# Rotary scores on one core: which ring carries the loads of q and k

## The chip, the cores and the metric

The kernel runs on one core of a Trainium2 chip. The core has five engines that run on their own: TensorE (PE, matrix products and transposes), VectorE (DVE), ScalarE (ACT), GpSimd (POOL) and SyncE (SP, which here only issues transfers). Transfers between the chip's memory (HBM) and the on-chip tiles are carried by 16 DMA engines. An engine that issues a transfer puts it on a ring of its own: in the profile q1 is SyncE's, q10 ScalarE's and q0 GpSimd's. All three are served by the same 16 DMA engines.

The metric is the device time of one execution in microseconds (us); lower is better. Three runs of the kernel before gave 802.26, 803.96 and 805.82 us; the median is 803.96.

## What is computed

q and k have the shape (16, 512, 16, 64): batch, position, head, dimension, in 32-bit floats. Both are rotated by cosines and sines of the position, and for each batch and head all scores of q against k are returned:

```python
q_rot = np.concatenate([q1 * cos_q - q2 * sin_q,
                        q1 * sin_q + q2 * cos_q], axis=-1)
k_rot = np.concatenate([k1 * cos_q - k2 * sin_q,
                        k1 * sin_q + k2 * cos_q], axis=-1)
scores = np.einsum('bshd,bthd->bsht', q_rot, k_rot)
```

q1, q2, k1 and k2 are the two halves of the last dimension. The output has the shape (16, 512, 16, 512): 268.44 MB are written and 67.24 MB read.

## The kernel before

**Tiling.** The 512 positions of a batch are laid on 128 partitions, four to a partition (C = 4): position 4p + c stands on partition p in row c. The work is cut into NST = 64 steps, four to a batch; step i computes, for batch i // 4 and row i % 4, the scores of 128 positions of q with all 512 of k, for all 16 heads. These go into one stage tile (`st`, 128 partitions of 32 KB, 4 MB), of which there are three (NST_BUFS), used in turn. When the eight head pairs of a step are copied there, one 4 MB store writes the tile out.

**A step** (the loop at L488, from the fifth step on). For each head pair p, `scores` (L396) records two matrix products (L413) into a PSUM tile `ps`, one of three, and ScalarE's copy of it into the stage tile (L422). Between them stand, for rows that later steps need, the transposes on TensorE (L364) of rotated q (one step ahead) and k (four steps, one batch, ahead), with the copies out of PSUM (L382): q's by VectorE after p = 1 and 3, k's by ScalarE after p = 5 and 6. VectorE rotates in place in the input tiles, q two steps ahead and k five (`rope`, L316, instructions at L339). The first four steps handle batch 0 in small pieces, with stores of 1 MB.

**Input tiles.** q and k have two tiles each of 128 partitions by 16 KB (2 MB, a whole batch), used in turn: batch b goes into tile b % 2. A load may begin when the rows that it overwrites have been read by TensorE's transposes. For k of batch b + 2 that is by the end of step 4b - 1, the last one of batch b - 1; for q of batch b + 2 it is in step 4b + 2 for the last row.

**The loads before.** From the fifth step on SyncE issues a load of q or k as two of 1 MB, each holding two of the four rows, with a semaphore of its own: `load(which, b, half)` at L264. The calls stand at the ends of the steps, behind the step's store: the first half of k after step 4b - 1, its second after step 4b, the halves of q after steps 4b + 1 and 4b + 2 (L486 and L511 to L518). So each step puts a 4 MB store and a 1 MB load on SyncE's ring, where they are served in that order. The loads of k and q for batches 1 and 2 (L445, L446 and L479) are whole.

**The four GpSimd loads.** RELIEVED (L260) names four loads of q, of batches 5, 8, 11 and 14. GpSimd issues 120 partitions of these, in packets of 8 KB, and the rest of eight partitions goes on SyncE's ring (for two of them) or GpSimd's (for the other two). They are issued after steps 14, 26, 38 and 50, when TensorE has read the rows.

**What sets the order.** Every operation is recorded in a list by `Plan.add`; `Plan.resolve` (L38) works out which semaphores each must wait for, and `Plan.emit` (L96) writes each engine's program in recorded order. An operation of an engine therefore starts after the earlier ones of that engine, and a DMA issue holds up what follows it on the issuing engine. All transfers go through `dma` (L236), whose `dma_start` the profile shows as L237, whatever engine issues. The engine is the first argument; waits that the issuing engine knows to be over are left out.

Of the kernel before, what the change touches and what calls it, by code (L numbers as in the profile page):

```python
# [7 lines left out]
PE, ACT, DVE, POOL, SP = "PE", "ACT", "DVE", "POOL", "SP"  # L8
# [170 lines left out]
def kernel(  # L179
# [8 lines left out]
    nc = tc.nc  # L188
# [4 lines left out]
    B, S, H, D = q.shape  # L193
    HD = D // 2
    P = 128
    C = S // P
# [9 lines left out]
    dram = {  # L206
        "q": q.rearrange("b (p c) h d -> b p c h d", c=C),
        "k": k.rearrange("b (p c) h d -> b p c h d", c=C),
    }
# [19 lines left out]
    def one(f):  # L229
        def emit():  # L230
            a = f()
            return a, a

        return emit

    def dma(engine, e, dst, src, sem, reads=(), writes=(), also=()):  # L236
        plan.add(engine, one(lambda: e.dma_start(dst, src)), reads, writes, sem=sem, also=also)  # L237
# [22 lines left out]
    RELIEVED = {("q", 5): 0, ("q", 8): 1, ("q", 11): 2, ("q", 14): 3}  # L260
    tiny = [0]
    SLOW = 4

    def load(which, b, half=None):  # L264
        if b >= B:
            return
        t = inb[which][b % 2]
        sem = f"in_{which}{b % 2}"
        rows = [("in", which, b % 2, c) for c in range(C)]
        rest = [("in rest", which, b % 2, c) for c in range(C)]  # L270
        if (which, b) not in RELIEVED:
            lo, hi = (0, C) if half is None else (half * C // 2, (half + 1) * C // 2)
            dma(
                SP, nc.sync, t[:, lo:hi].rearrange("p c (h d) -> p c h d", h=H), dram[which][b][:, lo:hi],
                sem if half is None else f"{sem}_{half}", writes=rows[lo:hi] + rest[lo:hi],
            )
            return

        n, E, F = 120, C * H * D, C * H * D // 2
        x = RELIEVED[which, b]
        d = dram[which][b]

        def move_cursor(k):
            y = tiny[0]
            tiny[0] += 1
            src = bass.AP(q.tensor, 512 * y, [(512, k), (64, 2), (1, 2)])
            dst = scratch[:k, 4 * y : 4 * y + 4].rearrange("p (a b) -> p a b", a=2)  # L290
            dma(POOL, nc.gpsimd, dst, src, "cursor", writes=[("scratch", y)])

        def halves(lo, hi, keys, sem):
            src = bass.AP(d.tensor, d.offset + lo * E + F, [(E, hi - lo), (-F, 2), (1, F)])
            v = t[lo:hi]
            dst = bass.AP(v.tensor, v.offset + F, [(v.ap[0][0], hi - lo), (-F, 2), (1, F)])
            dma(POOL, nc.gpsimd, dst, src, sem, writes=keys)

        plan.add(POOL, None, (), rows)
        if x % 2:  # L300
            move_cursor(8)
            halves(n, P, rest, f"rest{x}")
        move_cursor(SLOW + 1)
        halves(0, n, rows, f"part{x}")
        if not x % 2:
            dma(SP, nc.sync, t[n:].rearrange("p c (h d) -> p c h d", h=H), d[n:], sem, writes=rest)
# [9 lines left out]
    def rope(which, n):  # L316
        if n < C:
            x = units[which, n]
            sv, k1, k2 = "p c (g j) -> p c g j", {"j": HD}, {"j": D}
            cs = cos_t.unsqueeze(2).to_broadcast((P, C, 2 * G, HD))  # L320
            ss = ss_v.unsqueeze(2).to_broadcast((P, C, G, D))
            pv = part.rearrange("p (c g j) -> p c g j", c=C, j=D)
            x5 = x.rearrange("p c (h x j) -> p c h x j", x=2, j=HD)
            p5 = part.rearrange("p (c h x j) -> p c h x j", c=C, x=2, j=HD)
            adds = [(x5[:, :, :, y], p5[:, :, :, 1 - y]) for y in range(2)]
        else:
            x = inb[which][n // C % 2][:, n % C]
            sv, k1, k2 = "p (g j) -> p g j", {"j": HD}, {"j": D}
            cs = cos_t[:, n % C].unsqueeze(1).to_broadcast((P, 2 * H, HD))
            ss = ss_v[:, n % C].unsqueeze(1).to_broadcast((P, H, D))  # L330
            pv = part.rearrange(sv, **k2)
            x4 = x.rearrange("p (h x j) -> p h x j", x=2, j=HD)
            swapped = bass.AP(part.tensor, part.offset + HD, [part.ap[0], (D, H), (-HD, 2), (1, HD)])
            adds = [(x4, swapped)]
        xs, xc = x.rearrange(sv, **k2), x.rearrange(sv, **k1)
        keys, more = src_keys(which, n), src_also(which, n)

        def tt(o, a, b, op, reads, writes):
            plan.add(DVE, one(lambda: nc.vector.tensor_tensor(o, a, b, op=op)), reads, writes, also=more)  # L339

        def products():
            tt(pv, xs, ss, mult, keys + ["ss"], ["part"])
            tt(xc, xc, cs, mult, keys + ["cos"], keys)

        def sums():
            for y, z in adds:
                tt(y, y, z, add, keys + ["part"], keys)

        return [products, sums]
# [34 lines left out]
    def stage_of(i):  # L384
        return i % 2 if i < C else (i - 2) % NST_BUFS
# [4 lines left out]
    def ps_of(i, p):  # L390
        m = HP * i + p if i < FIRST else HP * ((i - FIRST) % PERIOD) + p
        if i >= FIRST and m >= HP * PERIOD - 3:
            return (1, 2, 1)[m - (HP * PERIOD - 3)]
        return m % NPS

    def scores(i, p):  # L396
        y, s = ps_of(i, p), stage_of(i)
        ps, st = ps_s[y], stage[s]
        b = i // C
        if b == 0:  # L400
            c, hp = divmod(p, 2)
            lhs, rhs = qTb[i % 2][:, C * hp + c], kTb[0][:, 2 * i + hp]
            keys = [("qT", i % 2, C * hp + c)] + [("kT", 0, 2 * i + hp, x) for x in range(C)]
        else:
            lhs, rhs = qTb[i % 2][:, p], kTb[b % 2][:, p]
            keys = [("qT", i % 2, p)] + [("kT", b % 2, p, x) for x in range(C)]

        def emit():
            done = []
            for r in range(2):  # L410
                lo, hi = 64 * r, 64 * r + 64
                done.append(
                    nc.tensor.matmul(out=ps[:, r, :], lhsT=lhs[lo:hi, :], rhs=rhs[lo:hi, :], start=True, stop=True)  # L413
                )
            return done[0], done[-1]

        plan.add(PE, emit, keys, [("ps", y)])
        so, si = st[:, 2 * p : 2 * p + 2, :], ps
        if b > 0:
            so = so.rearrange("s r (t c) -> s r t c", c=C)  # L420
            si = si.rearrange("s r (c t) -> s r t c", c=C)
        plan.add(ACT, one(lambda: nc.scalar.copy(out=so, in_=si)), [("ps", y)], [("st", s, p)])  # L422
        if b == 0 and p % 2 == 1:
            c = p // 2
            dma(
                SP, nc.sync, o_v[0, c, :, G * i : G * (i + 1)], st[:, G * c : G * (c + 1)], f"out{s}_{c}",
                reads=[("st", s, p - 1), ("st", s, p)],
            )
        elif b > 0 and p == HP - 1:
            dma(SP, nc.sync, o_v[b, i % C], st, f"out{s}", reads=[("st", s, x) for x in range(HP)])  # L430
# [5 lines left out]
    def run(ops):  # L436
        for op in ops:
            op()
# [3 lines left out]
    for head, heads in ((0, G), (G, H - G)):  # L442
        load_units("k", head, heads)
        load_units("q", head, heads)
    load("k", 1)  # L445
    load("q", 1)  # L446
    plan.add(POOL, one(lambda: nc.gpsimd.memset(ident, 0.0)), (), ["ident"])
    plan.add(
# [15 lines left out]
    for i in range(C):  # L464
# [18 lines left out]
                dve = dve[m:]  # L483
                tr_act(*nxt.pop(0))
        run(dve)
    load("k", 3, 0)  # L486

    for i in range(C, NST):  # L488
        plan.step = i
        tr = {}  # L490
        if i + 1 < NST:
            tr[1], tr[3] = ("q", i + 1, 0), ("q", i + 1, 1)
        if i + C < NST:
            tr[5], tr[6] = ("k", i + C, 0), ("k", i + C, 1)
        dve = []
        if i + 2 < NST:
            dve += rope("q", i + 2)
        if i + 1 + C < NST:
            dve += rope("k", i + 1 + C)
        for p in range(HP):  # L500
            scores(i, p)
            if p not in tr:
                continue
            if tr[p][0] == "q":
                run(dve[:1])
                dve = dve[1:]
                transposed(*tr[p], DVE)
            else:
                transposed(*tr[p], ACT)
        run(dve)  # L510
        if i % C == 0:  # L511
            load("k", i // C + 2, 1)
        elif i % C == C - 1:
            load("k", i // C + 3, 0)
        elif ("q", i // C + 2) not in RELIEVED:
            load("q", i // C + 2, i % C - 1)
        elif i % C == C - 2:
            load("q", i // C + 2)  # L518

    plan.resolve()  # L520
# [34 lines left out]
```

## Time and profile before

| What | Value | Where from |
|---|---|---|
| Time, three runs | 802.26, 803.96, 805.82 us | times |
| The profiled execution: time, span | 802.26 us, 800.5 us | times, page |
| Mean granted TensorE clock | 0.945 of full speed | times |
| TensorE busy (matrix products) | 680.5 us, 85% | page, part 1 |
| ScalarE busy | 561.6 us, 70% | page, part 1 |
| VectorE busy | 545.2 us, 68% | page, part 1 |
| DMA, whole span | 335.88 MB, mean 420 GB/s | page, part 3 |
| SyncE waiting for ScalarE's copies | 714.4 us, 76 times | waits of SyncE's queue |
| SyncE waiting for the last store | 21.1 us | waits of SyncE's queue |

The page's second part cuts the span in 40 slices of 20 us. A digit there is the busy share of an engine in tenths; the row DMA is the mean of the 16 DMA engines, and the row GB/s what they moved. The chain of waits (part 4) follows the work that ended last back to its cause, step by step. In the list of groups (part 5) a line ends with the idle time just before its instructions and what ended it. Part 6 gives for each kind of transfer the number, the size and the median time from issue to landing.

The trace also holds every DMA packet with queue, size and duration. The large ones of the kernel before:

```
queue         packet, bytes  packets  median ns  what
SyncE (q1)    32768          7680     1213       stores of 4 MB
SyncE (q1)    16384          528      612        whole loads, and small rests
SyncE (q1)    8192           7680     309        half loads; stores of 1 MB
GpSimd (q0)   8192           992      309        the four loads of q
```

### The profile page before, as it was taken

To read this page: it belongs to the slowest core of one execution; us is meant where nothing else is said; L and a number is where in the kernel's file an instruction comes from. 1 tells how busy PE (TensorE), PEld (TensorE's weight loads), DVE (VectorE), ACT (ScalarE), POOL (GpSimd) and SP (SyncE) were. 2 spreads that over 40 slices of the span, in tenths; PEclk is the share of its full clock that TensorE was granted. 3 is DMA by queue.
4 is the path that set the end of the run, shared out by engine and by line. 5 is a ranking of instruction groups with operands and counts; after the bars stand their busy time and mean duration, and the time that the engine had idled before them with its cause. 6 is when DMAs were issued, how large, how long until landed. Compare 5 with 4: busy or idle time off the path is not lost.

```text
span 800.5 us, 8241 instructions
## 1 busy us (share of the span) xinstructions
PE 680.5 (85%) x3072; PEld 292.0 (36%) x3072; DVE 545.2 (68%) x516; ACT 561.6 (70%) x647; POOL 8.4 (1%) x18
## 2 busy tenths in 40 slices
PE   3989999889699898869998988798889879989960
PEld 2444443334243333324343333343333324334420
DVE  6999988657487686648866765587767648775300
ACT  2978887867488668658786684687766658768870
POOL 0000000000000000100000000000000100000000
PEclk9999999989899999989999998899999989999995
DMA  9999999999999999999999999999999999999997
GB/s 350 419 424 414 386 436 421 438 424 401 429 429 430 436 428 434 389 436 431 430 431 432 429 432 383 432 432 428 434 433 427 380 438 427 431 432 426 433 431 306
DMA packets 21682, 335.88 MB, mean 420 GB/s; under 512 B 2480, under 2 KB 3760, under 8 KB 4784
## 3 DMA queue, kind: packets, MB, share of 16 engines
q1 hardware_dynamic: 20000, 327.43, 96.5%
q0 software_dynamic: 1376, 8.13, 2.8%
q10 hardware_dynamic: 288, 0.13, 0.1%
q8 instruction: 6, 0.10, 0.0%
q14 instruction: 12, 0.10, 0.0%
HBM read 67.24 MB, written 268.44 MB: 419 GB/s over the span
## 4 chain that ended last, share of the span: by engine, by line
DMA 52%; PE 31%; DVE 8%; ACT 5%; issue 1%; ACTq 0%; DVEq 0%; SPq 0%
DMA out_dram<-st 51%; PE ps L413 24%; PE bank L364 8%; ACT st L422 5%; DVE st L339 3%; DVE part L339 2%; DVE k_sb L339 2%; DVE q_sb L339 1%; DMA sin_t<-in_sin_dram 1%; DVE kT L382 0%; DVE qT L382 0%; ACTq L237 0%; ACT ss_t L459 0%; ACT ss_t L458 0%; ACTq L110 0%
## 5 line engine op out<-in xcount | busy, mean ns | idle before, releaser
L422 ACT COPY st<-ps 128x1024 f32<-128x1024 f32 x512 | 494.6, 1020 | 200.0 <-DMA out_dram<-st 124.8
L413 PE MATMUL ps<-kT,qT 64*128 64x512 f32 x2048 | 540.0, 641 | 77.9 <-ACT st L422 77.8
L413 PEld LDWEIGHTS ps<-kT,qT 64*128 64x128 f32 x2048 | 179.3, 193 | 269.4 <-ACT st L422 139.1
L382 DVE COPY qT<-bank 128x512 f32<-128x512 f32 x118 | 81.6, 692 | 199.5 <-PE bank L364 199.5
L364 PEld LDWEIGHTS bank<-ident,q_sb 128*128 128x128 f32 x480 | 54.0, 148 | 99.3 <-issue 94.3
L364 PE MATMUL bank<-ident,q_sb 128*128 128x128 f32 x480 | 84.6, 302 | 1.0 <-DVE q_sb L339 1.0
L364 PEld LDWEIGHTS bank<-ident,k_sb 128*128 128x128 f32 x480 | 50.4, 141 | 94.1 <-DVE k_sb L339 45.9
L364 PE MATMUL bank<-ident,k_sb 128*128 128x128 f32 x480 | 78.7, 287 | 1.6 <-DVE qT L382 0.8
L382 ACT COPY kT<-bank 128x512 f32<-128x512 f32 x122 | 72.7, 599 | 6.7 <-PE bank L364 6.7
L339 DVE TENSOR_TENSOR part<-q_sb,ss_t 128x1024 f32<-128x1024 f32 x60 | 73.5, 1225 | 3.7
L339 DVE TENSOR_TENSOR q_sb<-q_sb,cos_t 128x1024 f32<-128x1024 f32 x60 | 73.5, 1225 | 2.1
L339 DVE TENSOR_TENSOR k_sb<-k_sb,part 128x1024 f32<-128x1024 f32 x60 | 73.5, 1225 | 2.1
L339 DVE TENSOR_TENSOR k_sb<-k_sb,cos_t 128x1024 f32<-128x1024 f32 x60 | 73.5, 1225 | 2.0
L339 DVE TENSOR_TENSOR part<-k_sb,ss_t 128x1024 f32<-128x1024 f32 x60 | 73.0, 1216 | 0.3
L339 DVE TENSOR_TENSOR q_sb<-q_sb,part 128x1024 f32<-128x1024 f32 x60 | 72.9, 1216 | 0.0
L364 PE MATMUL bank<-ident,st 128*128 128x128 f32 x64 | 10.8, 318 | 14.2 <-DVE st L339 14.2
L364 PEld LDWEIGHTS bank<-ident,st 128*128 128x128 f32 x64 | 8.2, 161 | 19.5 <-DVE st L339 17.7
L339 DVE TENSOR_TENSOR part<-st,ss_t 128x1024 f32<-128x1024 f32 x8 | 9.8, 1223 | 7.4 <-ACT ss_t L459 7.0
L339 DVE TENSOR_TENSOR st<-st,part 128x512 f32<-128x512 f32 x16 | 11.1, 691 | 0.5
L237 POOL DMA_DIRECT2D scratch<-in_q_dram x6 | 3.6, 601 | 617.0 <-PE bank L364 617.0
L339 DVE TENSOR_TENSOR st<-st,cos_t 128x1024 f32<-128x1024 f32 x8 | 9.8, 1225 | 0.3
L382 ACT COPY qT<-bank 128x512 f32<-128x512 f32 x10 | 5.7, 618 | 3.5 <-PE bank L364 3.5
(11 smaller groups left out, 11.0 us busy)
## 6 DMA issues: line engine op xcount, KB each, us to landing
out_dram<-st SPq DMA_DIRECT2D x60, 4096.0 KB, 25.7
k_sb<-in_k_dram SPq DMA_DIRECT2D x26, 1024.0 KB, 28.6
q_sb<-in_q_dram SPq DMA_DIRECT2D x18, 1024.0 KB, 27.2
out_dram<-st SPq DMA_DIRECT2D x16, 1024.0 KB, 12.0
q_sb<-in_q_dram POOLq DMA_DIRECT2D x4, 1920.0 KB, 30.9
k_sb<-in_k_dram SPq DMA_DIRECT2D x2, 2048.0 KB, 13.7
q_sb<-in_q_dram SPq DMA_DIRECT2D x2, 2048.0 KB, 15.4
st<-in_k_dram SPq DMA_DIRECT2D x1, 1536.0 KB, 9.0
```

The costliest lines, as they stand in the source:

```text
L237: plan.add(engine, one(lambda: e.dma_start(dst, src)), reads, writes, sem=sem, also=also)
L339: plan.add(DVE, one(lambda: nc.vector.tensor_tensor(o, a, b, op=op)), reads, writes, also=more)
L364: done = [nc.tensor.transpose(bank[:, x, :], srcs[x], ident) for x in range(4)]
L382: plan.add(engine, one(lambda: copy(out=dst, in_=src)), [("bank", m)], keys)
L413: nc.tensor.matmul(out=ps[:, r, :], lhsT=lhs[lo:hi, :], rhs=rhs[lo:hi, :], start=True, stop=True)
L422: plan.add(ACT, one(lambda: nc.scalar.copy(out=so, in_=si)), [("ps", y)], [("st", s, p)])
```

## The change

The loads of 2 MB are no longer cut in two. ScalarE issues them, in its own program, after the third copy (p = 2) of a step: k of batch b + 2 in step 4b, and q of batch b + 2 in step 4b + 3. The load after the fourth step (the first half of k for batch 3) is gone; that k is now loaded whole in the fifth step. The four GpSimd loads, their rests, and all stores stay where they were, and so do the startup loads, for which `load` is still called with SyncE.

In the program of the changed kernel SyncE has 44 transfers fewer and ScalarE 22 more, each between two copies of L422, and none of the 22 has a semaphore wait of its own.

```diff
-    def load(which, b, half=None):
+    def load(which, b, engine=SP):
...
         if (which, b) not in RELIEVED:
-            lo, hi = (0, C) if half is None else (half * C // 2, (half + 1) * C // 2)
-            dma(
-                SP, nc.sync, t[:, lo:hi].rearrange("p c (h d) -> p c h d", h=H), dram[which][b][:, lo:hi],
-                sem if half is None else f"{sem}_{half}", writes=rows[lo:hi] + rest[lo:hi],
-            )
+            e = nc.sync if engine == SP else nc.scalar
+            dma(engine, e, t.rearrange("p c (h d) -> p c h d", h=H), dram[which][b], sem, writes=rows + rest)
             return
...
-    load("k", 3, 0)
...
             scores(i, p)
+            if p == 2 and i % C == C - 1 and ("q", i // C + 2) not in RELIEVED:
+                load("q", i // C + 2, ACT)
+            elif p == 2 and i % C == 0:
+                load("k", i // C + 2, ACT)
...
-        if i % C == 0:
-            load("k", i // C + 2, 1)
-        elif i % C == C - 1:
-            load("k", i // C + 3, 0)
-        elif ("q", i // C + 2) not in RELIEVED:
-            load("q", i // C + 2, i % C - 1)
-        elif i % C == C - 2:
+        if i % C == C - 2 and ("q", i // C + 2) in RELIEVED:
             load("q", i // C + 2)
```

## The prediction

> **What bounds the kernel now.** I read the page's slices first, then its queue table, then the chain, then the waits, and last the busy table over chosen stretches.
>
> ```profile
> PE   3989999889699898869998988798889879989960
> ACT  2978887867488668658786684687766658768870
> DMA  9999999999999999999999999999999999999997
> GB/s 350 419 424 414 386 436 421 438 424 401 429 429 430 436 428 434 389 436 431 430 431 432 429 432 383 432 432 428 434 433 427 380 438 427 431 432 426 433 431 306
> ...
> q1 hardware_dynamic: 20000, 327.43, 96.5%
> q0 software_dynamic: 1376, 8.13, 2.8%
> ...
> DMA 52%; PE 31%; DVE 8%; ACT 5%; issue 1%; ACTq 0%; DVEq 0%; SPq 0%
> ...
> L422 ACT COPY st<-ps 128x1024 f32<-128x1024 f32 x512 | 494.6, 1020 | 200.0 <-DMA out_dram<-st 124.8
> ...
> out_dram<-st SPq DMA_DIRECT2D x60, 4096.0 KB, 25.7
> k_sb<-in_k_dram SPq DMA_DIRECT2D x26, 1024.0 KB, 28.6
> q_sb<-in_q_dram SPq DMA_DIRECT2D x18, 1024.0 KB, 27.2
> q_sb<-in_q_dram POOLq DMA_DIRECT2D x4, 1920.0 KB, 30.9
> ```
>
> The DMA engines are 90% busy or more in all slices but the last, so 335.88 MB over the rate is nearly the time. Stores-only slices near the end run at about 432 GB/s; 335.88 MB at 432 is 777.5 us. The span is 800.5, so some 23 us lie between it and a faultless stream. About 2.0 are the empty start and 2.5 the end after the last packet; 2.7 more are engines that ran out between 790 and 798. The rest is lost rate, and the row GB/s says where: the first slice, then slices 5, 10, 17, 25 and 32 (386, 401, 389, 383, 380), while their neighbours hold 420 to 438.
>
> ScalarE waited 124.8 us for a stage tile to be stored, TensorE behind it: compute runs ahead and is held by the stores. Where nothing holds it, the stores leave SyncE 10.02 us apart (218.98, 229.00, 239.02 in the timeline), and a 4 MB store at 432 takes 9.7. So what moves the end is DMA time alone: an order of transfers changes nothing unless it changes the rate or empties the queue.
>
> I looked at the weak slices with the busy table (start:end, length, engines, TensorE clock, DMA share, GB/s):
>
> ```profile
> 86.00:96.00 10.00, 10.00 (x51) 4.41 (x50) 9.67 (x10) 8.67 (x11) 0.00 (x0) 1.00 0.90 339
> 186.00:196.00 10.00, 8.20 (x40) 3.27 (x38) 6.52 (x7) 6.79 (x8) 0.00 (x0) 1.00 1.03 383
> 196.00:206.00 10.00, 5.45 (x28) 2.22 (x24) 5.50 (x5) 2.92 (x4) 0.00 (x0) 1.00 1.02 437
> 332.00:342.00 10.00, 8.46 (x42) 3.63 (x40) 6.34 (x7) 6.86 (x9) 0.00 (x0) 1.00 1.01 359
> 480.00:490.00 10.00, 6.99 (x30) 2.70 (x26) 3.94 (x4) 5.24 (x6) 0.00 (x0) 0.82 1.00 333
> 630.00:640.00 10.00, 6.38 (x24) 2.77 (x24) 4.42 (x6) 4.34 (x5) 0.00 (x0) 0.83 1.01 332
> ```
>
> The share stays near 1.0 while the rate falls: the engines are occupied by slow packets. The packets by queue tell which. GpSimd's queue carries its four loads at 187 to 209, 334 to 362, 480 to 501 and 629 to 657 us. SyncE's 8 KB packets (the half loads of k) lie at 185 to 195, 332 to 342, 478 to 491 and 625 to 639. Each dip is the overlap of the two and ends with the k load: afterwards GpSimd's load runs on beside stores at full rate (196 to 206: 437; by packets 431 from 195 to 209, stores 351 and GpSimd 79). In the overlaps an 8 KB packet of k takes 373 to 484 ns on average, against 309 elsewhere. The dip at 86 has one load only: after the queue had run empty at 76 all 16 engines read the same half load at once, 435 ns a packet.
>
> **The change part by part.** Removed: 44 SyncE loads of 1 MB (26 of k, 18 of q). Added: 22 loads of 2 MB (13 and 9) on ScalarE's ring, with no wait of their own in its program. Kept: stores, startup loads, the GpSimd loads and the small SyncE rest of those.
>
> 1. Packet size. A half load has 8 KB a partition, a whole one 16 KB. Median packets: 309 ns for 8 KB, 612 for the 16 KB of the whole loads near the start. 44 x 128 x 309 ns = 1740 us of engine time against 22 x 128 x 612 = 1723; over 16 engines **1.1 us** saved. The tiny packets that signal completion (9 ns) count for nothing.
>
> 2. The dip at 86 us. From 86 to 92 the packets moved 305 GB/s: 6 x (1 - 305/432) = **1.8 us** lost. Whole 16 KB loads with all engines reading ran at 428 to 430 (15 to 23 us), and the third k load now runs beside stores, so I count all of it saved; bounds 0 and 2.
>
> 3. The four GpSimd overlaps. By the table 10 x (1 - rate/432): 1.1 + 1.7 + 2.3 + 2.3 = **7.4 us** lost. Now k's load is issued in step 4b after the third copy and is served at once instead of behind some 24 us of queue. The k load that collided (first packet at 185, asked for at 161) would be over by then; but the next one, in step 16, starts near 193 and meets the tail of GpSimd's load. Then every engine takes 32 KB of stores, 16 of k and 8 of q in turn: that packets are taken in turn shows in 351 to 79 GB/s above, about 32 to 8. Reads are then 24 of 56, some 186 GB/s. Elsewhere 245 GB/s of reads beside 185 of stores ran unhindered (470 us, half loads); in the dips reads of 150 to 240 did not. Bounds: all 7.4 stay, or none. I take a fifth as left, since stores now always hold over half of each engine, nearer to the row of 195 to 209: **6.0** saved.
>
> 4. Two rings at other times. A load beside stores gets 16 of 48 KB, so 2.10 MB at 144 GB/s takes 14.6 us; 22 of them are 321 us with two rings drawn from. The nearest row, GpSimd's load beside stores, is 431 against 432 to 433. But half loads behind stores on one ring, engines out of step, also gave 431 (366 to 480 us). I count **-0.3**; bounds +1 and, by the slowest two-ring row (332), 321 x 100/432 = -74, which that row's full-rate tail makes remote.
>
> 5. The queue early on. It ran dry from 74 to 78 us (301 GB/s there, 1.2 us lost). The third k load, asked for at about 70 instead of 65 and 76, fills that; but with nothing behind store 4 the queue may empty when store 5 is issued at 86.2, until the q load in step 7 (near 100). Bounds -1 and +1.2; **+0.2**.
>
> 6. ScalarE's issuing. 22 issues; SyncE's take 0.34 to 1.2 us, median 0.49, so 11 us in all and at most 26, in ScalarE's own order: the copy behind it is late, then TensorE for a bank. It is free, as ScalarE is busy 70% and the step ends with a store that queues anyway; two stores in the queue cover 19 us. Without that cover it is 11 us.
>
> 7. Lateness. k is first needed near step 4b+3, 2.9 steps or 35 us on; q 2.8 steps, 33 us. At 14.6 us, or 17 with three in turn, neither is late. A store beside a load takes 14.6 instead of 9.7, so stage tiles come free later in the loading steps and sooner in the others; the queue still holds two stores, more than a step of compute. SyncE's stores lose 44 issues in front of them, worth nothing, as SyncE waited 714 us for ScalarE.
>
> Sum: 1.1 + 1.8 + 6.0 - 0.3 + 0.2 = **8.8 us**. Span 791.7; the profiled execution took 802.26 for a span of 800.5, so 793.5. It was the fastest of three; from the median 803.96 it gives **795**.
>
> The Trainium skill speaks against this change: "DMA: Bandwidth & Descriptors", section "Rules for kernel authors", says that spreading DMAs over the issuing engines brings no bandwidth, only the time to issue. By it alone the sum would hold items 1 and 5, some 803. The flat 431 of GpSimd's tail agrees that a second ring adds no rate; what I count is who meets whom.
>
> **The rivals.** *The dips stay*: they belong to GpSimd's loads starting, and k merely suffers. For it: all four begin as that load begins. Against: each ends with the k load, whatever its length, and 86 us has a dip without GpSimd. Saving 2.8: 801. *Two rings are slower*: reads and stores drawn packet by packet lower the rate wherever a load runs. For it: slices 10, 17, 25 and 32. Against: 437 in 196 to 206. It decides below 432 x (1 - 8.8/321) = 420 GB/s in those 321 us; at the 401 of slice 10 it costs 321 x 31/432 = 23 us, the dips stay as well, and the time is 804 - 2.8 + 23 = 824. *ScalarE's issuing shows*: the cover of item 6 is gone in compute-bound steps and the dips stay: 804 - 2.8 + 11 = 812. For it: steps at 10.02 us; against: 124.8 us of waiting for stores.
>
> **How the numbers follow.** Forecast 0.56, dips stay 0.21, two rings slower 0.18, issuing 0.05. About 0.5% (4 us) is what this kernel's runs can tell from no change. The forecast is faster (790 to 799 by its bounds), with a sliver of the first rival; that rival is otherwise no change; the last two are slower. Faster 0.57, same 0.21, slower 0.22. The range takes in the forecast and the first rival, with the spread of runs: 790 to 806.
>
> **What would show it.** Slices 5, 17, 25 and 32 above 420 show items 2 and 3; if they stay below 400 with no k load there, the first rival. A rate under 425 in all loading stretches shows the second; ScalarE's wait for stores well under 124.8 with gaps in the DMA row, the third. A ScalarE queue (q10) with some 46 MB shows that the loads moved. Wrong altogether if TensorE waits for k or q.

## The result, and the profile after

The changed kernel took 797.77 us (median of four runs, 797.40 to 798.30), the kernel before 803.66 (four runs, 802.26 to 805.82). The ratio is 0.9925 with a 95% interval of 0.9902 to 0.9948: 5.9 us faster, where the prediction had 8.8. Timed again twice, beside the experiments, the ratio was 0.9933 (0.9910 to 0.9956) and 0.9943 (0.9923 to 0.9963). The profiled executions lie 4.7 us apart by span (800.5 and 795.8).

These lines of the page of the changed kernel answer to those shown of before: the rates in 40 slices, the queues, the chain, ScalarE's copies and one line of VectorE's rotation, and the transfers (number, KB each, median us to landing).

```profile
DMA  8999999999999999999999999999999999999997
GB/s 344 420 425 432 432 423 437 422 435 420 404 435 430 433 427 428 436 416 420 432 427 430 423 429 429 397 428 436 429 430 432 433 421 427 431 432 432 433 427 303
...
q1 hardware_dynamic: 13664, 281.29, 83.0%
q10 hardware_dynamic: 3456, 46.27, 13.8%
q0 software_dynamic: 1376, 8.13, 2.6%
...
DMA 48%; PE 35%; DVE 8%; ACT 5%; issue 1%; ACTq 0%; DVEq 0%; SPq 0%
...
L419 ACT COPY st<-ps 128x1024 f32<-128x1024 f32 x512 | 494.9, 1020 | 196.2 <-DMA out_dram<-st 121.0
...
L336 DVE TENSOR_TENSOR part<-q_sb,ss_t 128x1024 f32<-128x1024 f32 x60 | 73.5, 1225 | 12.6 <-DMA q_sb<-in_q_dram 9.7
...
out_dram<-st SPq DMA_DIRECT2D x60, 4096.0 KB, 25.5
k_sb<-in_k_dram ACTq DMA_DIRECT2D x13, 2048.0 KB, 23.1
q_sb<-in_q_dram ACTq DMA_DIRECT2D x9, 2048.0 KB, 19.0
...
q_sb<-in_q_dram POOLq DMA_DIRECT2D x4, 1920.0 KB, 38.7
```

The loads have moved (46.27 MB on q10, ScalarE's ring). DMA still bounds the kernel, and ScalarE still waits 121.0 us for stores (124.8 before). Slice 5 is repaired: 386 to 432. The other weak slices have moved one slice on, the first as deep as it was and the others shallower: 401, 389, 383 and 380 in slices 10, 17, 25 and 32 have turned into 404, 416, 397 and 421 in slices 11, 18, 26 and 33. The busy table of the changed kernel over chosen stretches (start:end, length, the engines, TensorE clock, DMA share, GB/s) shows where these dips stand:

```profile
86.00:96.00 10.00, 10.00 (x50) 4.43 (x48) 9.32 (x9) 8.67 (x11) 0.00 (x0) 1.00 1.00 428
190.00:200.00 10.00, 10.00 (x50) 4.17 (x46) 8.53 (x9) 7.40 (x9) 0.00 (x0) 1.00 1.03 433
205.00:215.00 10.00, 6.99 (x34) 2.93 (x32) 7.00 (x7) 4.45 (x6) 0.00 (x0) 1.00 1.01 385
354.00:364.00 10.00, 7.72 (x38) 3.17 (x37) 6.70 (x6) 6.25 (x9) 0.00 (x0) 1.00 0.99 394
486.00:496.00 10.00, 9.64 (x48) 4.04 (x44) 8.53 (x9) 7.45 (x10) 0.00 (x0) 1.00 1.01 426
500.00:510.00 10.00, 6.87 (x34) 2.94 (x32) 6.89 (x7) 4.33 (x6) 0.00 (x0) 1.00 0.96 379
```

By the packets of the trace GpSimd's loads run from 190 to 217, 340 to 375, 484 to 512 and 634 to 669 us, and the k loads that they meet begin at 205, 355, 500 and 650. In the rows at 190 and 486, beside stores alone, the rate is 433 and 426; it falls when k joins. By packets some 1.2 us of the loss in the four stretches stand before k's first packet and some 4.2 behind it, so most of a dip begins with the second load, not with GpSimd's. But two loads in flight together are not enough for a dip. In the second stretch k's load runs until 373 and GpSimd's until 375, and the rate comes back while both are in flight:

```profile
355.00:362.00 7.00, 5.66 (x28) 2.22 (x24) 5.70 (x6) 3.25 (x6) 0.00 (x0) 1.00 0.95 377
362.00:370.00 8.00, 7.06 (x34) 3.24 (x36) 4.27 (x4) 7.64 (x10) 0.00 (x0) 1.00 1.02 434
```

The second half of the overlap ran at 426 and 427 GB/s by packets in the second and fourth stretch, and at 384 and 359 in the first and third, where SyncE's rest of eight partitions is read as well (212 to 218 and 509 to 513 us). Two more profiles of the changed kernel, taken beside the experiments, divide in the same way (418 to 428 against 344 to 390). No run here takes that rest away, so its part in the dips is not tested. Over the whole of these four stretches the two kernels show (before first, then changed):

```profile
187.00:209.00 22.00, 12.74 (x62) 5.16 (x58) 11.05 (x11) 9.91 (x13) 0.00 (x0) 0.94 1.01 408
334.00:362.00 28.00, 19.53 (x84) 7.92 (x81) 13.99 (x15) 14.62 (x18) 0.00 (x0) 0.88 1.02 410
480.00:501.00 21.00, 17.16 (x68) 6.72 (x64) 12.49 (x12) 10.26 (x12) 0.00 (x0) 0.84 1.01 387
629.00:657.00 28.00, 18.51 (x72) 7.55 (x70) 11.84 (x12) 13.05 (x15) 0.00 (x0) 0.82 1.01 398
```

```profile
190.00:217.00 27.00, 20.40 (x98) 8.51 (x94) 18.00 (x17) 16.09 (x19) 0.00 (x0) 0.96 1.01 406
340.00:375.00 35.00, 30.69 (x144) 12.86 (x144) 22.07 (x21) 24.93 (x29) 0.00 (x0) 1.00 1.01 421
484.00:512.00 28.00, 21.93 (x104) 9.32 (x104) 18.92 (x18) 17.38 (x20) 0.00 (x0) 1.00 1.01 402
634.00:669.00 35.00, 31.18 (x134) 13.04 (x134) 23.19 (x22) 25.11 (x29) 0.00 (x0) 0.90 1.01 425
```

Length times (1 - rate / 432), summed, is 7.0 us lost before and 5.0 after. Counted from the packets themselves, which puts each byte where it moved, the span divides like this. Each entry is the DMA time lost against 432 GB/s in that part, as a mean over the 16 engines:

```
                                        before  changed
0 to 15 us                               4.1     4.3
74 to 92 us                              3.2     0.2
GpSimd's four stretches                  7.9     5.5
the rest, to 25 us before the end        3.0     3.2
last 25 us: engines that ran out         2.5     2.7
after the last packet                    2.7     2.7
```

So the profiled 4.7 us are 3.0 around 86 us and 2.4 in GpSimd's stretches, less some 0.6 elsewhere. That leaves nothing for the smaller number of SyncE issues, and ScalarE's 22 issues of 0.33 us each cost nothing visible.

### The profile page after: what moved, and what is told of

The parts are those of the page before. It is cut to its first block, busy times and chain, and to the rows that moved or that the text cites. A ratio compares the mean times of both kernels' runs of the same rounds, so it can differ in the third digit from the quotient of the medians.

```text
span 795.8 us, 8197 instructions
## 1 busy us (share of the span) xinstructions
PE 680.6 (86%) x3072; PEld 293.3 (37%) x3072; DVE 545.0 (68%) x516; ACT 561.8 (71%) x647; POOL 8.4 (1%) x18
## 3 DMA queue, kind: packets, MB, share of 16 engines
q10 hardware_dynamic: 3456, 46.27, 13.8%
## 4 chain that ended last, share of the span: by engine, by line
DMA 48%; PE 35%; DVE 8%; ACT 5%; issue 1%; ACTq 0%; DVEq 0%; SPq 0%
DMA out_dram<-st 48%; PE ps L410 27%; PE bank L361 8%; ACT st L419 5%; DVE st L336 3%; DVE part L336 2%; DVE k_sb L336 2%; DVE q_sb L336 1%; DMA st<-in_k_dram 1%; DVE kT L379 0%; DVE qT L379 0%; ACTq L110 0%; DVEq L110 0%; SPq L544 0%; SPq L515 0%
## 5 line engine op out<-in xcount | busy, mean ns | idle before, releaser
L419 ACT COPY st<-ps 128x1024 f32<-128x1024 f32 x512 | 494.9, 1020 | 196.2 <-DMA out_dram<-st 121.0
L336 DVE TENSOR_TENSOR part<-q_sb,ss_t 128x1024 f32<-128x1024 f32 x60 | 73.5, 1225 | 12.6 <-DMA q_sb<-in_q_dram 9.7
L336 DVE TENSOR_TENSOR k_sb<-k_sb,cos_t 128x1024 f32<-128x1024 f32 x60 | 73.5, 1225 | 2.0
L336 DVE TENSOR_TENSOR q_sb<-q_sb,cos_t 128x1024 f32<-128x1024 f32 x60 | 73.5, 1225 | 2.1
L336 DVE TENSOR_TENSOR k_sb<-k_sb,part 128x1024 f32<-128x1024 f32 x60 | 73.5, 1225 | 2.1
L336 DVE TENSOR_TENSOR st<-st,cos_t 128x1024 f32<-128x1024 f32 x8 | 9.8, 1225 | 0.3
## 6 DMA issues: line engine op xcount, KB each, us to landing
k_sb<-in_k_dram ACTq DMA_DIRECT2D x13, 2048.0 KB, 23.1
q_sb<-in_q_dram POOLq DMA_DIRECT2D x4, 1920.0 KB, 38.7
```

## The experiments

Two questions were open: which part of the change gains (whole loads, their places, or the ring), and why the repaired overlaps bring less than they should. The end of the kernel is set by the last of the 16 DMA engines, so beside the time this table gives the **lag**: the time from the median engine's completion of a store to the last engine's, taken from the completion marks that each engine leaves, for the stores nearest to these moments.

```
store near (us)             187  334  482  630  680  last
before                      3.6  4.0  3.1  3.3  1.4  1.6
changed                     2.0  4.7  2.2  3.8  1.7  2.8
changed, beside e11, e10    2.1  3.2  1.0  3.2  2.2  2.3
changed, beside e4          2.4  4.5  4.2  4.3  3.5  3.9
whole, SyncE's ring (e11)   5.2  4.0  4.6  5.4  3.6  5.7
k later (e10)               2.3  4.3  4.4  4.6  3.6  5.6
no GpSimd loads (e4)        2.6  5.1  7.9  8.0  8.0  9.1
GpSimd in 16 KB (e5)        1.9  4.8  7.2  8.8  8.7  8.2
```

The three profiles of the changed kernel lie up to 3.2 us apart at one store (1.0 to 4.2 near 482) and 1.6 at the end. Smaller differences between versions say nothing.

**The ring.** The loads stay whole, but SyncE issues them. In SyncE's program their order against the stores is that of the changed kernel's places.

```diff
-            if p == 2 and i % C == C - 1 and ("q", i // C + 2) not in RELIEVED:
-                load("q", i // C + 2, ACT)
-            elif p == 2 and i % C == 0:
-                load("k", i // C + 2, ACT)
...
-        if i % C == C - 2 and ("q", i // C + 2) in RELIEVED:
+        if i % C == C - 2:
             load("q", i // C + 2)
+        elif i % C == C - 1:
+            load("k", i // C + 3)
```

and `load("k", 3)` before the loop. Expected:

> The loads whole (2 MB) but on SyncE's ring, at the earliest places (q after step 4b+2, k after step 4b-1). No second hardware ring, but the queue of some 24 us puts k's loads before and after GpSimd's. If the gain comes from which reads meet: GpSimd's stretches lose under 2 us in all (5.8 in the changed kernel, 8.0 in the one before), the stretch from 86 us loses nothing, and the time is 793 to 796, below the changed kernel. If the gain comes from ScalarE's ring as such: 801 to 804, as before.

Measured: 798.85 us, ratio 0.9933 (0.9916 to 0.9950). Half of the first expectation held: the overlaps are gone (1.0 us lost by packets). The other half did not: the time is not below the changed kernel's. So it was run again beside that kernel, on one chip.

> Whole loads on SyncE's ring, beside the changed kernel: the only difference is the ring, with what follows from it (which loads meet GpSimd's). If the ring is worth nothing: within 1 us of the changed kernel (797 to 800), and with less scatter (under 3 us from lowest to highest). If the ring matters: 2 us or more above.

> The changed kernel as it stands, timed on the same chip as the three above, which are to be read against it: 797 to 799.

Measured: 798.66 us (797.76 to 799.62), ratio 0.9947 (0.9929 to 0.9966); the changed kernel 798.31 (796.53 to 800.01), ratio 0.9943. The two rings end alike. In this version k also no longer meets GpSimd's loads, so a gain of the ring could be hidden by one of the places; the ring alone is tried below, with halves, and brings nothing either. GpSimd's stretches in this version, by the busy table:

```profile
186.00:208.00 22.00, 15.55 (x67) 6.47 (x68) 11.31 (x12) 12.54 (x14) 0.00 (x0) 0.84 1.00 427
332.00:362.00 30.00, 24.63 (x108) 9.96 (x104) 19.52 (x19) 17.61 (x21) 0.00 (x0) 0.94 1.00 428
480.00:502.00 22.00, 16.88 (x68) 7.15 (x70) 10.89 (x11) 12.74 (x14) 0.00 (x0) 0.84 1.01 432
628.00:656.00 28.00, 24.56 (x103) 10.04 (x100) 17.68 (x17) 18.89 (x22) 0.00 (x0) 0.88 1.01 430
```

They hold 427 to 432: by packets 0.9 us lost instead of 7.9. Yet the span is 796.4. The missing time stands elsewhere: 4.9 us in the rest between 92 us and the last 25 (2.0 before, 2.7 in the changed kernel beside it), and 5.2 us of engines that ran out (2.5 and 2.1). The last lines of the busy table show that, first for this version, then for the changed kernel on the same chip:

```profile
785.00:790.00 5.00, 0.00 (x0) 0.00 (x0) 0.00 (x0) 0.00 (x0) 0.00 (x0) 0.50 0.53 229
790.00:795.00 5.00, 0.00 (x0) 0.00 (x0) 0.00 (x0) 0.00 (x0) 0.00 (x0) 0.50 0.08 33
```

```profile
785.00:790.00 5.00, 0.00 (x0) 0.00 (x0) 0.00 (x0) 0.00 (x0) 0.00 (x0) 0.50 0.97 419
790.00:795.00 5.00, 0.00 (x0) 0.00 (x0) 0.00 (x0) 0.00 (x0) 0.00 (x0) 0.50 0.17 72
```

From 785 to 790 half of the engines are already done in the one, nearly none in the other, and both end at about 794. Of the completion marks of the last store the middle ones came at 788.5 and 791.6, the last at 794.2 and 793.9: the median engine gained 3.1 us, the last one nothing. Why the rest loses more here is not known.

**Halves.** First the ring with the half loads and places of before: in `load` of the kernel before, `SP, nc.sync` becomes `ACT, nc.scalar` where `half` is given.

> The ring alone: the half loads of 1 MB at the places of the kernel before, issued by ScalarE. If it is which reads meet: the halves of k are asked for after steps 4b-1 and 4b, are served at once and lie inside GpSimd's loads, so the four stretches still lose 4 to 8 us, and 8 KB packets cost 1 us more: 798 to 802. If the ring alone gives the gain: 797 to 798.

Measured: 803.68 us, ratio 0.9994 (0.9975 to 1.0013): no gain, and above both ranges expected. Then the changed kernel with each load cut in two at its place:

```diff
-            dma(engine, e, t.rearrange("p c (h d) -> p c h d", h=H), dram[which][b], sem, writes=rows + rest)
+            for x in (range(2) if engine == ACT else ()):
+                lo, hi = x * C // 2, (x + 1) * C // 2
+                dma(
+                    engine, e, t[:, lo:hi].rearrange("p c (h d) -> p c h d", h=H), dram[which][b][:, lo:hi],
+                    f"{sem}_{x}", writes=rows[lo:hi] + rest[lo:hi],
+                )
```

> The changed kernel with each of its 22 loads cut into two of 1 MB again, issued one after the other at the same place by ScalarE. If whole loads (16 KB packets) are what gained: 801 to 804. If place or ring gained: 797 to 799.

> The changed kernel once more, beside the next ones on one chip: 797 to 799 if its first time was typical; 800 to 804 if two-ring kernels scatter as the later-k version did (798.8 to 805.3).

Measured on one chip: 801.34 us, ratio 0.9975 (0.9954 to 0.9996), against 798.13, ratio 0.9933 (0.9910 to 0.9956). Cutting the loads at the same place on the same ring costs some 3.2 us; the two intervals just touch, but all ten runs with halves took 799.86 or more and six of the seven beside them 799.17 or less. What the halves keep of the gain, 801.34 against 803.95 for the kernel before on that chip, is 2.6 us, with an interval just clear of no change, and belongs to the new places (the halves at the old places on the same ring brought nothing). By packets the halves lose no more in GpSimd's stretches (5.2 us against 5.6) but more in the rest (5.8 against 2.6; the profiled execution with halves took 803.23, above its median): outside those stretches 137 store packets took over 1400 ns (median 1213), 65 in the changed kernel's first profile and 74 in its last.

**The meeting of k and GpSimd's load.** The four k loads that meet one are asked for a step later; nothing else changes.

```diff
-            elif p == 2 and i % C == 0:
+            elif p == 2 and i % C == (("q", i // C + 1) in RELIEVED):
                 load("k", i // C + 2, ACT)
```

> The changed kernel, with only the four loads of k that meet GpSimd's load asked for one step later (step 4b+1). If reads that meet are the loss: the four stretches lose 1 to 2 us instead of 5.8, and the time is 793 to 795. If GpSimd's loads are slow by themselves: 797 to 798, no change. If k then comes late (about 30 us to its first use, 23 from issue to landing): VectorE waits for k_sb and the time is 799 or more.

Measured: 802.88 us (798.83 to 805.28), ratio 0.9976 (0.9958 to 0.9994). The time is above all that was expected without VectorE waiting for k. Again, beside the changed kernel:

> The later k once more, now beside the changed kernel on one chip. If reads that meet cost the end: at least 1 us below the changed kernel. If they only slow DMA engines that have time in hand, since one slow engine sets the end: not below the changed kernel (797 to 804). If its first 802.88 was the chip: within 1 us of the changed kernel.

Measured: 802.92 us (800.03 to 806.71), ratio 0.9994 (0.9977 to 1.0012), against 0.9943: slower by 4 to 5 us, twice. No engine waits for k_sb in its profile; VectorE waits 10.0 us for q_sb, against 6.1 in the changed kernel beside it. Its GpSimd stretches, now almost free of k:

```profile
189.00:213.00 24.00, 21.77 (x104) 9.20 (x102) 18.91 (x18) 17.38 (x20) 0.00 (x0) 1.00 1.00 419
339.00:370.00 31.00, 29.77 (x141) 12.45 (x138) 22.93 (x22) 25.47 (x30) 0.00 (x0) 1.00 1.00 416
488.00:510.00 22.00, 20.53 (x98) 8.58 (x94) 18.27 (x18) 15.98 (x20) 0.00 (x0) 1.00 1.01 418
636.00:667.00 31.00, 29.21 (x139) 12.22 (x138) 22.34 (x21) 24.91 (x29) 0.00 (x0) 1.00 1.00 415
```

The deep dips are gone, but the stretches run at 415 to 419 on average, not at 430; by packets they still lose 4.0 us (6.0 in the changed kernel beside it). The gain of 2.0 there is given back: 4.7 us in the rest instead of 2.7, 5.5 of engines that ran out instead of 2.1. One idea is that the meeting holds up the engines that lead. The lag does not settle it: across the second GpSimd load, between the stores at 334 and 384, it shrinks from 4.3 to 3.7 here, and in the three profiles of the changed kernel from 4.7 to 1.6, from 3.2 to 1.4 and from 4.5 to 3.6. Why the last engine itself finishes 3.7 us later than in the changed kernel (797.6 and 793.9) is not settled.

**The engine that lags.** GpSimd's loads hold 120 of the 128 partitions, and small transfers ahead of them (`move_cursor` in the kernel) shift where their shares begin; the intent is that one DMA engine (`SLOW`) gets no part of them. The trace does not number the engines, so this cannot be seen directly. Here is the changed kernel without GpSimd's loads, so that ScalarE loads those q too:

```diff
-    RELIEVED = {("q", 5): 0, ("q", 8): 1, ("q", 11): 2, ("q", 14): 3}
+    RELIEVED = {}
```

> The changed kernel without GpSimd's four loads: ScalarE loads these q as well. If the end is set by one slow DMA engine that GpSimd's loads spare: the other engines end at 788 to 790, the slow one 8 to 12 us after them, time 800 to 808. If GpSimd's loads only cost their overlaps: no dips, time 791 to 793.

Measured: 803.57 us, ratio 1.0004 (0.9987 to 1.0021): all of the gain is gone, as the first expectation had it. The lag grows to 7.9 us by 482 and 9.1 at the end, and the last lines of its busy table show a few engines working alone:

```profile
785.00:790.00 5.00, 0.00 (x0) 0.00 (x0) 0.00 (x0) 0.00 (x0) 0.00 (x0) 0.50 0.87 374
790.00:795.00 5.00, 0.00 (x0) 0.00 (x0) 0.00 (x0) 0.00 (x0) 0.00 (x0) 0.50 0.30 131
795.00:800.00 5.00, 0.00 (x0) 0.00 (x0) 0.00 (x0) 0.00 (x0) 0.00 (x0) 0.50 0.08 33
```

Its median engine ends at 790.5, like the changed kernel's 790.7 on the same chip, without a single overlap; its last ends at 799.5 instead of 794.7. It is not one engine alone: half of the engines end by 789.8, and the second-last is still 6.5 us behind the median. So GpSimd's loads more than pay for their dips, and the lag shows where: at the engines that end last. That it is the spared engine that ends last without them is argued from the kernel, not seen. The version with GpSimd's packets of 16 KB (a partition's 16 KB in one run, where `halves` swaps the two 8 KB) was meant for the pattern of the reads:

> The changed kernel, with GpSimd's loads in packets of 16 KB (a partition's rows in one piece) instead of two of 8 KB. If the pattern of 8 KB halves is what collides: the overlaps lose under 2 us in all, time 793 to 796, though reads hold half of the engines (32 of 64 KB in turn) instead of 24 of 56. If the share of reads decides: the overlaps lose as much or more than 5.8 us, time 797 to 800.

Measured: 809.18 us, ratio 1.0067 (1.0049 to 1.0084). Neither expectation: the lag climbs to 8.8 us, with the second-last engine 2.6 behind the median at the end, as if this form no longer spared the engine that lags. But the median engine ends 6 us later too (796.8 against 790.8), with twelve of the engines within 0.2 us of each other, so the lag is not all of it. The run says nothing on the pattern. Last, a fifth such load (q of batch 15 added to RELIEVED), on SyncE's ring and in the changed kernel:

> The version with whole loads on SyncE's ring, and a fifth load by GpSimd (q of batch 15). If the slowest engine's lag (5 us behind the median in that version) sets the end: it falls to 2 to 3 us and the time is 795 to 798. If GpSimd's loads only cost: 799 to 801.

> The changed kernel with a fifth GpSimd load (q of batch 15). If the slow engine's lag at the end (3 to 4 us) sets the time: 1 to 2 us less, 796 to 797. If not: 798 to 799.

Measured: 797.88 us, ratio 0.9925 (0.9910 to 0.9940), with a lag of 3.4 at the end, and 798.87, ratio 0.9965 (0.9939 to 0.9990), with 2.1. The first is on a par with the changed kernel timed beside it (798.13) and cannot be told from whole loads on SyncE's ring without the fifth load (ratios 0.9933 and 0.9947). The second is not below the changed kernel (798.31), which is the branch expected if the lag does not set the time; its lag of 2.1 against 2.3 had hardly moved, so it does not decide. No version tried beats the changed kernel beyond the intervals.

## Why the prediction was right, and where not

*The bound* was read rightly: DMA ends the kernel, and waits of the other engines hide behind it. But the working counted **mean** lost rate over 16 engines as time of the end. That holds only where all lose alike. The version without overlaps lost 0.9 us there instead of 7.9 and ended no earlier than the changed kernel; the engines that were helped finished early and stood idle.

*Item 1, packet size (1.1 us)*, was mis-sized: halves at the same place and ring cost about 3.2 us (801.34 against 798.13). The packet medians were right (611 ns for 16 KB), but halves also go with more slow store packets beside them.

*Item 2, the dip at 86 us (1.8)*: right; the stretch from 86 to 96 went from 339 to 428 GB/s. *Item 5, the early queue (+0.2)*: 1.0 by packets, since the pause that was feared at 86 did not come.

*Item 3, the overlaps (6.0 of 7.4)*, is the term that failed: 2.0 by the table, 2.4 by packets. The step that failed is "I take a fifth as left": some 70% was left. The share on which the step rests came out about as forecast: while k and GpSimd's load ran together, reads took 172 and 179 GB/s of 413 and 418 in the second and fourth stretch and 199 and 189 of 389 and 376 in the others, 42 to 51% against the forecast 43% (24 of 56). The rate did not follow from it. The row chosen for it, GpSimd's load beside stores alone, was the wrong neighbour. The sign named for it was a poor one as well: slices 5, 17, 25 and 32 did rise above 420 (432, 436, 429 and 433), because the dips had moved to the next slices. With 2.4 for item 3 the sum would have been 5.2, near the 5.9 measured, but the version on SyncE's ring shows that the method would not have been right by that: there nearly all of item 3 was gained, and the end did not move.

*Item 4 (two rings, -0.3)* agrees with the runs, as far as they can tell so small a term: 798.66 on one ring, 798.31 on two. The rule of the Trainium skill ("DMA: Bandwidth & Descriptors", section "Rules for kernel authors"), that spreading transfers over issuing engines brings no bandwidth, agrees with these two times. *Item 6*: 22 issues of 0.33 us, free as said. *Item 7*: ScalarE's loads landed after 23.1 and 19.0 us instead of 14.6 and were in time; but GpSimd's, now sharing with two rings, went from 30.9 to 38.7 us, and VectorE waited for q_sb twice, 6.6 us at 375 and 3.1 at 670. Behind the stores this cost nothing that can be seen.

*The rivals.* "The dips stay" was wrong in its mechanism for the changed kernel, since they begin for the most part with k, but half right in its number; and the later k shows that GpSimd's load beside stores alone can also run at 415 to 419. "Two rings are slower" and "issuing shows" did not happen. The forecast was right in sign and in what bounds the kernel; its gain was 5.9 of 8.8. That the sum came this near is in part luck: item 1 was too small by some 2 us and item 3 too large by some 3.6, and the two partly cancel.

## What to carry over

When transfers bound a kernel as here, it ends with its last DMA engine, so price a change by what that engine gains, not by the mean rate: look at how far the engines' completions of one transfer lie apart, and whether it shrinks or grows. A second issuing ring brought nothing here; undivided loads and better places did. The loads that share the engines unevenly were worth their own dips: without them the last engine fell further behind. Two loads in flight together were often slower than a load beside a store, though not always, so watch which transfers meet, but check that the engines that are slowed set the end.

## What was not expected of the hardware

Without GpSimd's loads the last engine fell behind by up to 9.1 us over the run, and the second-last by 6.5. In the changed kernel's stretch of stores alone from 725 to 780 us 5.4% of the 32 KB packets (one engine of 16 would be 6.2%) took 1225 ns or more, 1274 on average, at a median of 1213; but in the kernel before it was 8.9%, and without GpSimd's loads 12.7%, so that they are the packets of one engine is not shown. A half load of k beside GpSimd's load brought the rate down to 332 GB/s, and one read in part with no store beside it to 305 from 86 to 92 us (295 by packets from 88 to 90, where it ran alone); a whole load of k beside GpSimd's ran at 377 and then at 434 in the changed kernel, while a GpSimd load beside stores ran at 431 in the kernel before and at 415 to 419 in the later-k version. What sets this is open.
